# Attention scores over all 128 rows, another start order and other buffers for the conv weights

## The chip, the cores and the metric

The kernel runs on one core of a Trainium2 chip. The metric is the device time of one execution in microseconds (us), the median of three runs. The engines are called PE (TensorE, matrix products), DVE (VectorE), ACT (ScalarE), POOL (GpSimd) and SP (SyncE, which issues most loads). PEld is PE's loading of stationary weights.

## The reference, cut to what matters

One decoder block over 1024 tokens of width 1024: a combined projection, a gated short convolution and a sliding-window attention side by side, their gated sum, and a gated MLP with a convolution.

```python
u  = RMSNorm(x)
cb, cc, cx, q, k, v, g_conv, g_attn = split(u @ W_in + b_in)
y_conv = (cb * causal_dwconv3(cc * cx)) @ W_conv_out
y_attn = attention(rope(q), rope(k), v, sinks) @ W_attn_out + b
x = x + (sigmoid(g_conv) * y_conv + sigmoid(g_attn) * y_attn) @ W_mix_out
u  = RMSNorm(x)
up, gate = split(u @ W_up)
x = x + (silu(causal_dwconv3(up) + b) * gate) @ W_down
return RMSNorm(x)

# attention: 8 query heads, 2 key heads of 64; blocks of 128 queries;
# each block sees its own and the previous block of keys, band of 128
kk = concat([prev_block(k), k])            # block 0: the previous block is padding
scores = qb @ kk.T * 64 ** -0.5            # -inf outside the band and on the padding
m = max(max(scores), sink)
p = exp(scores - m); out = p / (sum(p) + exp(sink - m)) @ vv
```

## The kernel before

All arithmetic is float32. For PE each operand is split into a high part (an ACT cast) and a low part (a DVE subtraction), by `split`, and a product is three PE products, high by high, high by low and low by high (`mm3`, lines 144 to 146). So a weight tile of 128x1024 costs a load by SP into a buffer of the pool `rawp` (two buffers), a cast and a subtraction. Activation tiles of 128x1024 come from a pool of 16 buffers (`act`). Work runs in this order.

**The start** is written out by hand for all engines. For each of 8 blocks of 128 tokens, `rows_of(t)` makes the norm's statistics and the scaled rows y_a (five small DVE operations and one of 128x1024), and `cols_of(t)` turns them on PE (tp_a, line 182, 8 transposes) and splits the result into u. `part(name, qt)` (line 288) multiplies a weight tile (k, q0, q1) with 256 columns of u, 24 products; it needs two blocks of u. `turn_on(n)` lets the generator of the rotary angles go on by n operations, DVE ones first (lines 209 to 217), then 25 on POOL (lines 220 to 224), then DVE ones again. `keep_warm` runs products of zeros. In PSUM the accumulators of k, q0 and q1 (ps_k, ps_q) leave one place for tp_a.

**Attention** has 16 steps (8 query blocks by 2 key heads), `Step`, written out by hand for PE, ACT and DVE. Per step: a set of scores, four heads with two products each (lines 444 and 445); maxima with mask on DVE (451), exponentials on ACT, sums and normalised p on DVE (467); eight transposes of p (`turn`, 473); a split of these; four products with the values (483); then the head's output is summed and split into qs (`rest`, `total`, `store`). The first product of a score has the stationary qs[g], where the high and low part of one head's queries stand above each other in 64 rows each, and as moving side the high keys in both halves. The second has 64 rows, high queries by the low keys kl. Between a step's turn and its values PE runs half of a fill tile: 24 products with u (ps_fill), which make the attention gates and two tiles of the conv's input; DVE splits a fill weight in every second step.

**The attention output** (ya) multiplies W_ao with the attention's result, in the same tiles qs. After it comes the conv's in-projection with fewer products by a sum-and-difference scheme (zin, xin, yin), whose result z is stored to DRAM by column tiles.

**The conv output** (yc, line 144 ff. with co and z as operands) multiplies eight weight tiles co0 to co7 with z parts reloaded from DRAM (zr, halves of 512 tokens: z00 to z07, z10 to z17); the results are gated and merged (gm, line 917), split (m) and multiplied with eight mix weight tiles (mx). Here a scheduler sets the order, by when operands come and by the order of the code. Every weight tile and z part goes through the two buffers of `rawp`. Then come the MLP's up and down projections.

Of the kernel before, what the change touches and what calls it, by code (L numbers as in the profile page):

```python
# [72 lines left out]
def hybrid_kernel(ctx, tc, x, pos, cst, pcol, norms, w_in, w_ao, w_co, w_mix, w_up, w_down, out):  # L73
# [36 lines left out]
    def pc(i):  # L110
        return pcol_sb[:, i:i + 1]
# [129 lines left out]
    def turn_on(n=99):  # L241
        for _ in zip(range(n), angles):
            pass
# [32 lines left out]

    def cols_of(t, step=None):
        norm_cols(ys[t], u, t, f"a{t}", step)
# [12 lines left out]
    with tc.manual_schedule(engines={mybir.EngineType.PE, mybir.EngineType.Activation, mybir.EngineType.DVE, mybir.EngineType.SP, mybir.EngineType.Pool}):  # L291
        nc.vector.memset(eps, EPS)
        nc.scalar.activation(warm, eps, AF.Sqrt)
        nc.gpsimd.memset(zero, 0.0)
        keep_warm(N_WARM[0])
        load_x(0)
        nc.scalar.dma_start(posi, pos)
        nc.scalar.dma_start(cst_sb[:, CST_FREQ:CST_MASK], cst[:, CST_FREQ:CST_MASK])
        wb = act("nw0")
        nc.sync.dma_start(wb, norms[0:1, :].broadcast_to([P, D]))  # L300
        load_x(1)
        nc.sync.dma_start(cst_sb[:, :CST_FREQ], cst[:, :CST_FREQ])
# [21 lines left out]
        nc.sync.dma_start(cst_sb[:, CST_MASK:], cst[:, CST_MASK:])  # L324
        rows_of(2)
        turn_on(20)
        early["q0"] = split_unit(raw_q0, "q0")
        rows_of(3)
        part("k", 0)
        cols_of(2)  # L330
        early["q1"] = split_unit(raw_q1, "q1")
        rows_of(4)
        part("q0", 0)
        cols_of(3)
        rows_of(5)
        part("q1", 0)
        part("k", 1)
        cols_of(4)
        rows_of(6)
        part("q0", 1)  # L340
        cols_of(5)
        rows_of(7)
        turn_on(4)
        part("q1", 1)
        part("k", 2)
        cols_of(6)
        turn_on(7)
        part("q0", 2)
        cols_of(7)
        turn_on()  # L350
        part("q1", 2)
# [25 lines left out]

    own = [slice(0, HD), slice(HD, P)]
    other = [own[1], own[0]]
    qs = [mid(f"qs{g}", F32R) for g in range(2)]  # L380
    ks = [act(f"ks{g}", F32R) for g in range(2)]
    kl = act("kl", F32R)

    def rope_keys(part):
        k = rope(part)
        for g in range(2):
            split(k[own[g]], ks[g][own[g]], kl[own[g]])
        for g in range(2):
            nc.vector.tensor_copy(ks[g][other[g]], ks[g][own[g]].bitcast(F32))

    def rope_queries(part, c):
        q = rope(part)
        for g in range(2):
            split(q[own[g]], qs[g][own[g], c], qs[g][other[g], c])

    turn = {"k": rope_load(ps_early["k"], COL_BIN + U_K, "k")}
    for i in range(2):
# [24 lines left out]
    def fill_part(f, h, kcs):  # L422
        if h == 0 and kcs[0] == 0:
            ps_fill[f] = ps(f"ps_fill{f}")
        gemm_part(ps_fill[f], w_fill[f], u, halves[h], kcs)

    def fill_evict(f):
        col, alloc = fillers[f]
        filled[f] = alloc(f"fill{f}")
        return nc.scalar.activation(filled[f], ps_fill[f], AF.Identity, bias=pc(COL_BIN + col))  # L430

    class Step:
        def __init__(self, i):
            self.n, self.g = steps[i]
            self.name = f"{self.n}{self.g}"
            self.queries = slice(self.n * P, (self.n + 1) * P)

        def scores(self):
            rows, g = own[self.g], self.g
# [28 lines left out]

        def turn(self):
            self.pt = pt = ps(f"pt{self.name}", (P, 2, 4, P))  # L470
            for k2 in range(2):
                for c in range(4):
                    nc.tensor.transpose(pt[:, k2, c], self.p[:, c, k2 * P:(k2 + 1) * P], ident)

        def split(self):
            self.hl = [act(f"p{x}{self.name}", F32R, (P, 2, 4, P)) for x in "hl"]
            split(self.pt, *self.hl)
# [16 lines left out]

        def store(self):
            r = own[self.g]
            return split(self.os[r], qs[0][r, :, self.queries], qs[1][r, :, self.queries])

    for f in range(2):
        fill_split(f, load_unit(w_in[U_GA + f], f"fill{f}"))
# [11 lines left out]
    with tc.manual_schedule(engines={mybir.EngineType.PE, mybir.EngineType.Activation, mybir.EngineType.DVE}):  # L514
# [9 lines left out]
        for i, step in enumerate(st):  # L524
# [30 lines left out]
            if i == len(st) - 1:  # L555
                wa = [split_unit(raw_ao[0], "ao0")]
            step.values()
        st[-1].rest()
# [157 lines left out]
    v.scalar_tensor_tensor(c_0, ps_fill[9], pc(COL_BIN + U_X), c_0, op0=ALU.add, op1=ALU.mult)  # L716
    conv_taps(0, c_0)


    units_in = [(U_GC, U_B)]  # L720
# [55 lines left out]
    for q in range(4):  # L776
        if q > 1:
            wa.append(unit(w_ao[q], f"ao{q}"))
        if q > 1:
            next(gen_in)  # L780
            next(gen_in)
        if q == 3:
            pin.load(0)
            pin.prep(0, 3)
            pin.prep(0, 2)
        for jj in range(2):
            j = 2 * q + jj
            with tc.issue_after(after_attention):
                nc.scalar.activation(gas[j], gas[j], AF.Sigmoid)
            ya = ps(f"ya{j}")  # L790
            for cols in halves:
                for c in range(4):
                    f = slice((jj * 4 + c) * P, (jj * 4 + c + 1) * P)
                    mm3(ya[:, cols], wa[q][0][:, f], wa[q][1][:, f], qs[0][:, c, cols], qs[1][:, c, cols], c == 0, c == 3)
            v.scalar_tensor_tensor(ms[j], ya, pc(COL_BAO + j), gas[j], op0=ALU.add, op1=ALU.mult)
            nc.gpsimd.dma_start(msp[j], ms[j])
    wp.release()
    midp.release()
# [52 lines left out]
                3: [(2, lambda p: gate(p, bank("z"), pin.uv[p][:, 0]))]}.get(q, [])  # L851


    wco, zparts = {}, {}
# [12 lines left out]

    def tail_in(m):
        for f in {0: [lambda: load_co(0)], 1: [lambda: load_z(0, 0)], 2: [lambda: load_z(0, 1)], 3: [lambda: load_co(1)],
                  5: [lambda: load_co(2)], 6: [lambda: load_z(0, 2), lambda: load_z(0, 3)], 7: [lambda: load_co(3)]}.get(m, ()):  # L870
            f()

    pin.load(1)
# [446 lines left out]
```

## Time and profile before

| | |
|---|---|
| median of 3 runs | 1441.95 us (1440.77 to 1442.16) |
| profiled execution | 1441.58 us, span 1439.8 us |
| PE busy | 1418.2 us, 98% of the span |
| DVE busy | 1003.6 us, 70% |
| ACT busy | 562.5 us, 39% |
| POOL busy | 85.7 us, 6% |
| start, to the first 512-column product | 59.74 us |
| attention, first to last score | 109.6 to 255.6 us |
| conv and mix output | 601.7 to 710.9 us for the first 453 products |

The profile is of one execution; times in it count from the start of the span. [...] The granted clock is the share of full speed that PE was given.

### The profile page before, as it was taken

To read this page: it belongs to the slowest core of one execution; us is meant where nothing else is said; L and a number is where in the kernel's file an instruction comes from. 1 tells how busy PE (TensorE), PEld (TensorE's weight loads), DVE (VectorE), ACT (ScalarE), POOL (GpSimd) and SP (SyncE) were. 2 spreads that over 40 slices of the span, in tenths; PEclk is the share of its full clock that TensorE was granted. 3 is DMA by queue.
4 is the path that set the end of the run, shared out by engine and by line. 5 is a ranking of instruction groups with operands and counts; after the bars stand their busy time and mean duration, and the time that the engine had idled before them with its cause. 6 is when DMAs were issued, how large, how long until landed. Compare 5 with 4: busy or idle time off the path is not lost.

```text
span 1439.8 us, 17099 instructions
## 1 busy us (share of the span) xinstructions
PE 1418.2 (98%) x6447; PEld 1164.9 (81%) x6447; DVE 1003.6 (70%) x1511; ACT 562.5 (39%) x897; POOL 85.7 (6%) x144
## 2 busy tenths in 40 slices
PE   8999999999999999999999999999999999999997
PEld 6987777788888888877888878888888888888886
DVE  7575676856788787545644697787777777655567
ACT  5545555623333333232323543333333334444343
POOL 5210000000000000000000000000000000000000
PEclk9999999999999999999999999999999999999999
DMA  5320000242455554255552222222232225797603
GB/s 217 89 59 30 30 16 30 88 161 74 161 205 205 191 185 178 76 177 196 184 174 103 74 98 107 101 105 95 88 110 93 99 94 197 275 377 256 195 31 146
DMA packets 68450, 193.18 MB, mean 134 GB/s; under 512 B 8144, under 2 KB 8400, under 8 KB 68368
## 3 DMA queue, kind: packets, MB, share of 16 engines
q1 hardware_dynamic: 53280, 139.64, 28.8%
q0 software_dynamic: 14368, 51.13, 9.2%
q10 hardware_dynamic: 720, 1.33, 0.3%
q8 instruction: 50, 0.82, 0.2%
q14 instruction: 32, 0.26, 0.1%
HBM read 136.75 MB, written 52.69 MB: 132 GB/s over the span
## 4 chain that ended last, share of the span: by engine, by line
PE 86%; DVE 6%; DMA 5%; ACT 2%; issue 1%; SPq 0%; DVEq 0%; ACTq 0%
PE xup L649 8%; PE zup L649 8%; PE yup L649 8%; PE dna L1151 8%; PE dnb L1151 6%; PE yin L649 5%; PE xin L649 5%; PE zin L649 5%; PE wup L649 4%; PE win L649 3%; PE ps_fill L144 3%; PE ps_fill L146 3%; PE ps_fill L145 3%; PE mx L145 2%; PE mx L146 2%; PE mx L144 2%
## 5 line engine op out<-in xcount | busy, mean ns | idle before, releaser
L1138 DVE TENSOR_TENSOR pd<-rd,pd 128x1024 fp32r<-128x1024 f32 x77 | 93.7, 1222 | 54.1 <-ACT pd L1141 50.3
L627 ACT CAST pup<-sup 128x512 fp32r<-128x512 f32 x80 | 47.8, 620 | 203.2 <-DVE sup L613 203.2
L1141 ACT CAST pd<-rd 128x1024 fp32r<-128x1024 f32 x77 | 80.6, 1053 | 104.1 <-PE dnb L1151 37.1
L1151 PE MATMUL dna<-pd 128*128 128x512 f32 x528 | 120.3, 389 | 0.0
L1151 PEld LDWEIGHTS dna<-pd 128*128 128x128 f32 x528 | 99.1, 188 | 20.5
L1151 PE MATMUL dnb<-pd 128*128 128x512 f32 x396 | 90.2, 389 | 0.0
L1151 PEld LDWEIGHTS dnb<-pd 128*128 128x128 f32 x396 | 74.3, 188 | 15.4
L649 PE MATMUL zin<-u,pin 128*128 128x512 f32 x360 | 86.1, 389 | 0.0
L627 ACT CAST pin<-sin 128x512 fp32r<-128x512 f32 x52 | 31.1, 620 | 135.3 <-DVE sin L613 126.4
L649 PEld LDWEIGHTS zin<-u,pin 128*128 128x128 f32 x360 | 67.6, 188 | 14.0
L630 DVE TENSOR_TENSOR pup<-sup,pup 128x512 fp32r<-128x512 f32 x80 | 53.6, 689 | 18.5 <-ACT pup L627 15.0
L144 PE MATMUL ps_fill<-u,w_fill 128*128 128x512 f32 x160 | 64.0, 400 | 0.0
L146 PE MATMUL ps_fill<-u,w_fill 128*128 128x512 f32 x160 | 62.5, 391 | 0.0
L145 PE MATMUL ps_fill<-u,w_fill 128*128 128x512 f32 x160 | 62.3, 389 | 0.0
L649 PE MATMUL yup<-b22h,pup 128*128 128x512 f32 x176 | 57.9, 390 | 0.9 <-DVE aup L665 0.9
L649 PE MATMUL zup<-b11h,pup 128*128 128x512 f32 x176 | 57.8, 390 | 0.0
L649 PE MATMUL zup<-b21h,pup 128*128 128x512 f32 x176 | 57.7, 389 | 0.0
L451 DVE CUSTOM_DVE_ANT_0 p<-s,cst_sb,pcol_sb 128x256 f32<-128x256 f32 x64 | 27.2, 480 | 37.2 <-PE s L445 34.6
L649 PE MATMUL yup<-bt1h,pup 128*128 128x512 f32 x160 | 52.5, 389 | 0.0
L649 PE MATMUL wup<-bt2h,pup 128*128 128x512 f32 x160 | 52.5, 389 | 0.0
L649 PE MATMUL xup<-bt3h,pup 128*128 128x512 f32 x160 | 52.5, 389 | 0.0
L649 PE MATMUL xup<-bt4h,pup 128*128 128x512 f32 x160 | 52.5, 389 | 0.0
(361 smaller groups left out, 3470.4 us busy)
## 6 DMA issues: line engine op xcount, KB each, us to landing
rup<-in_w_up SPq DMA_DIRECT2D x44, 512.0 KB, 3.5
rin<-in_w_in SPq DMA_DIRECT2D x30, 512.0 KB, 6.7
td<-in_w_down SPq DMA_DIRECT2D x22, 512.0 KB, 5.3
tsp<-td POOLq DMA_DIRECT2D x22, 512.0 KB, 3.7
rd<-tsp SPq DMA_DIRECT2D x44, 256.0 KB, 5.3
rd<-in_w_down SPq DMA_DIRECT2D x33, 256.0 KB, 5.3
rd<-hs SPq DMA_DIRECT2D x33, 256.0 KB, 3.7
x<-in_x SPq DMA_DIRECT2D x16, 512.0 KB, 3.7
```

Of the source, the lines that this page charges most:

```text
L144: nc.tensor.matmul(dst, ah, bh, start=first, stop=False)
L145: nc.tensor.matmul(dst, ah, bl, start=False, stop=False)
L146: nc.tensor.matmul(dst, al, bh, start=False, stop=last)
L451: nc.vector.tensor_tensor_reduce(out=self.p[:, c], in0=self.s[:, c], in1=masks[0 if self.n == 0 else 1], scale=SCALE, scalar=pc(COL_SINK + ...
L627: nc.scalar.copy(self.parts[p, q][:, 0], src())
L630: v.tensor_sub(t[:, 1], src(), t[:, 0].bitcast(F32))
L649: nc.tensor.matmul(dst, a, b[:, kc], start=first and i == 0, stop=last and i == 2, skip_group_check=p >= PLAIN and more)
L1138: v.tensor_sub(t[:, 2:], raws_d[n - 1], t[:, :2].bitcast(F32))
L1141: nc.scalar.copy(parts_d[n][:, :2], raws_d[n])
L1151: nc.tensor.matmul(sets[side, i], t[:, s, tok], t[:, b], start=g == 0 and k == 0 and not more, stop=g == NG - 1 and k == 2, skip_group_che ...
```

## The change

1. **Scores.** The low keys become two tiles kl0 and kl1, one for each key head, of 128 rows; the other head's 64 rows are zeros, written once by POOL (two memsets of 64x1024). The second product of a score then runs over all 128 rows of qs[g], of which the zero rows add nothing.
2. **Queries by halves.** qs is laid out as halves of 512 tokens, then head, then token. W_ao's first group of products runs the first half for two output tiles and then the second half.
3. **First key block.** For query block 0 the two steps turn, split and multiply with the values only one key block (4 transposes and 2 value products a step instead of 8 and 4).
4. **First gate.** Fill 0 is stored to DRAM after its bias and reloaded later (ga0), which frees an activation buffer in between; the product that makes the conv's first input stands in the hand-written order, ahead of the last head's sum, and some work of the next stage is only issued after attention.
5. **Start.** x_1 is loaded ahead of the norm gains, q0's weights ahead of x_2. The first two blocks' norms come ahead of the angle operations; the first split of u comes behind eight of these; q0's weights are split ahead of block 2; the PE parts stand in another order.
6. **Conv weights.** co1 to co3 and z parts z00 to z03 are loaded into activation buffers and not through the two buffers of `rawp`.

```diff
+        load_x(1)
...
-        load_x(1)
         raw_k = load_unit(w_in[U_K], "k")
+        raw_q0 = load_unit(w_in[U_Q], "q0")
         load_x(2)
         load_x(3)
-        raw_q0 = load_unit(w_in[U_Q], "q0")
         load_x(4)
-        turn_on(2)
         rows_of(0)
-        turn_on(1)
         rows_of(1)
+        turn_on(8)
         cols_of(0, False)
         keep_warm(N_WARM[1])
+        early["k"] = split_unit(raw_k, "k", eng=nc.gpsimd)
         cols_of(0, True)
-        early["k"] = split_unit(raw_k, "k", eng=nc.gpsimd)
-        turn_on(5)
         cols_of(1)
+        turn_on(20)
...
-    qs = [mid(f"qs{g}", F32R) for g in range(2)]
+    qs = [mid(f"qs{g}", F32R, (P, 2, 4, 512)) for g in range(2)]
-    kl = act("kl", F32R)
+    kl = [act(f"kl{g}", F32R) for g in range(2)]
+    for g in range(2):
+        nc.gpsimd.memset(kl[g][other[g]].bitcast(F32), 0.0)
...
-                nc.tensor.matmul(self.s[:, c], qs[g][:, c, self.queries], ks[g][:, kc], start=True, stop=False)
-                nc.tensor.matmul(self.s[:, c], qs[g][rows, c, self.queries], kl[rows, kc], start=False, stop=True)
+                nc.tensor.matmul(self.s[:, c], qs[g][:, self.h, c, self.queries], ks[g][:, kc], start=True, stop=False)
+                nc.tensor.matmul(self.s[:, c], qs[g][:, self.h, c, self.queries], kl[g][:, kc], start=False, stop=True)
...
+            self.blocks = 2 if self.n else 1
-            for k2 in range(2):
+            for k2 in range(self.blocks):
                 for c in range(4):
                     nc.tensor.transpose(pt[:, k2, c], self.p[:, c, k2 * P:(k2 + 1) * P], ident)
...
-            for i in range(4):
-                nc.tensor.matmul(self.o, vs[self.g][:, n0 + i // 2], self.hl[i % 2][:, i // 2], start=i == 0, stop=i == 3)
+            n = 2 * self.blocks
+            for i in range(n):
+                nc.tensor.matmul(self.o, vs[self.g][:, n0 + i // 2], self.hl[i % 2][:, i // 2], start=i == 0, stop=i == n - 1)
...
+        if f == 0:
+            nc.gpsimd.dma_start(gsp0, filled[f])
...
+    gas[0] = act("ga0")
+    nc.sync.dma_start(gas[0], gsp0)
...
-        raw = load_unit(w_co[gr, hc], f"co{n}")
+        raw = raws_co.pop(n) if n in raws_co else load_unit(w_co[gr, hc], f"co{n}")
...
+    def fetch_co(n):
+        raws_co[n] = act(f"raw_co{n}")
+        nc.sync.dma_start(raws_co[n], w_co[n // 2, n % 2])
...
-        raw = rawp.tile([P, 512], F32, name=f"zr{th}{k}", tag="raw")
+        raw = rawp.tile([P, 512], F32, name=f"zr{th}{k}", tag="raw") if th or k > 3 else act(f"zr{th}{k}", F32, (P, 512))
```

The order of PE's work at the start, first before and then after. tp_a are the eight transposes of a token block (the order of the rows is that of blocks 2 to 6), ps_k, ps_q0 and ps_q1 the parts of 24 products; the first line is k's first part.

```order
L288 MATMUL ps_k_257<-u1_94,w_k_177 128x256 x24
L182 MATMUL tp_a2_282<-cst_sb_88,y_a2_212 128x128 x8
L288 MATMUL ps_q0_307<-u1_94,w_q0_243 128x256 x24
L182 MATMUL tp_a3_332<-cst_sb_88,y_a3_246 128x128 x8
L288 MATMUL ps_q1_354<-u1_94,w_q1_293 128x256 x24
L288 MATMUL ps_k_257<-u1_94,w_k_177 128x256 x24
L182 MATMUL tp_a4_403<-cst_sb_88,y_a4_296 128x128 x8
L288 MATMUL ps_q0_307<-u1_94,w_q0_243 128x256 x24
```

And after:

```order
L288 MATMUL ps_k_246<-u1_94,w_k_180 128x256 x24
L288 MATMUL ps_q0_282<-u1_94,w_q0_232 128x256 x24
L182 MATMUL tp_a2_307<-cst_sb_88,y_a2_235 128x128 x8
L182 MATMUL tp_a3_332<-cst_sb_88,y_a3_271 128x128 x8
L288 MATMUL ps_q1_343<-u1_94,w_q1_318 128x256 x24
L182 MATMUL tp_a4_379<-cst_sb_88,y_a4_321 128x128 x8
L288 MATMUL ps_k_246<-u1_94,w_k_180 128x256 x24
L182 MATMUL tp_a5_425<-cst_sb_88,y_a5_368 128x128 x8
L288 MATMUL ps_q0_282<-u1_94,w_q0_232 128x256 x24
```

q0's first part moved ahead of the turn of block 2, and k's second part behind the turn of block 4, so that the turns of blocks 2 and 3 follow each other and that of block 4 has one part ahead of it since block 3, not two.

The loads on SP at the entry of the conv output, first before and then after. raw_co are conv weight tiles, zr parts of z, gm gates for the merge.

```order
L121 DMA raw_co0_4601<-in_w_co 128x1024
L915 DMA gm00_4883<-gsp_2301 128x512
L916 DMA gm00_4883<-msp_2300 128x512
L864 DMA zr00_4624<-zsp_2302 128x512
L864 DMA zr01_4643<-zsp_2302 128x512
L121 DMA raw_co1_4661<-in_w_co 128x1024
L121 DMA raw_co2_4691<-in_w_co 128x1024
L864 DMA zr02_4699<-zsp_2302 128x512
L864 DMA zr03_4704<-zsp_2302 128x512
L121 DMA raw_co3_4712<-in_w_co 128x1024
L864 DMA zr04_4778<-zsp_2302 128x512
```

And after:

```order
L121 DMA raw_co0_4596<-in_w_co 128x1024
L880 DMA zr00_4619<-zsp_2298 128x512
L932 DMA gm00_4878<-gsp_2297 128x512
L933 DMA gm00_4878<-msp_2296 128x512
L876 DMA raw_co1_4624<-in_w_co 128x1024
L880 DMA zr01_4640<-zsp_2298 128x512
L876 DMA raw_co2_4645<-in_w_co 128x1024
L876 DMA raw_co3_4675<-in_w_co 128x1024
L880 DMA zr02_4693<-zsp_2298 128x512
L880 DMA zr04_4773<-zsp_2298 128x512
L880 DMA zr03_4701<-zsp_2298 128x512
L880 DMA zr05_4778<-zsp_2298 128x512
```

co1 to co3 (line 876 is the load into an activation buffer) moved up among the first z parts, and of the rows shown only co0, zr04 and zr05 still use the two buffers of `rawp`.

## Rows read from the trace of the kernel before

**Rows 1.** First part of the page: busy us (share) xinstructions, each engine.

```profile
PE 1418.2 (98%) x6447; PEld 1164.9 (81%) x6447; DVE 1003.6 (70%) x1511; ACT 562.5 (39%) x897; POOL 85.7 (6%) x144
```

**Rows 2.** Waits of PE: what waited for what, us in total, times, longest.

```profile
PE tp_a L182 <- DVE y_a L172: 3.6, 4, 1.6
PE yc L144 <- ACT co L138: 1.9, 1, 1.9
PE ps_k L288 <- DVE st_a L156: 1.5, 1, 1.5
...
PE yc L144 <- DVE gm L917: 1.1, 1, 1.1
PE ya L144 <- ACT qs L138: 1.0, 1, 1.0
```

**Rows 3.** Timeline of PE, one score set: start us, duration us, engine, line, operation.

```profile
117.60 0.28 PE L444 MATMUL s<-ks,qs 128*128 128x256 f32 x1
117.81 0.38 PE L445 MATMUL s<-kl,qs 64*128 64x256 f32 x1
118.12 0.39 PE L444 MATMUL s<-ks,qs 128*128 128x256 f32 x1
...
120.00 1.09 PE L473 MATMUL pt<-cst_sb,p 128*128 128x128 f32 x8
120.85 0.47 PE L144 MATMUL ps_fill<-u,w_fill 128*128 128x512 f32 x1
```

**Rows 4.** Chain that ended last, 35 to 45 us: start, us on it, what.

```profile
39.17 2.88 PE ps_k L288 x24
```

**Rows 5.** PEld, lines 445 and 288: duration ns minimum/median/maximum, first and last start.

```profile
L445 PEld LDWEIGHTS s<-kl,qs x64: 182/183/183, 109.8 to 255.6; 64*128 64x128 f32 x64
...
L288 PEld LDWEIGHTS ps_k<-u,w_k x96: 186/192/193, 13.8 to 52.0; 128*128 128x128 f32 x96
```

**Rows 6.** Timeline of PE, value products and the turn behind them, late in attention.

```profile
262.36 0.39 PE L483 MATMUL o<-ph,vs 128*128 128x512 f32 x1
...
263.27 1.03 PE L473 MATMUL pt<-cst_sb,p 128*128 128x128 f32 x8
264.06 0.48 PE L144 MATMUL ps_fill<-u,w_fill 128*128 128x512 f32 x1
```

**Rows 7.** Timeline of DVE over two attention steps; [ ] idle before and releaser.

```profile
178.37 0.48 DVE L451 CUSTOM_DVE_ANT_0 p<-s,cst_sb,pcol_sb 128x256 f32<-128x256 f32 x1 [1.50 <-PE s L445]
...
184.27 1.22 DVE L467 TENSOR_TENSOR p<-p,sm 128x1024 f32<-128x1024 f32 x1
188.08 0.48 DVE L451 CUSTOM_DVE_ANT_0 p<-s,cst_sb,pcol_sb 128x256 f32<-128x256 f32 x1 [2.58 <-PE s L445]
...
195.01 1.22 DVE L139 TENSOR_TENSOR w_fill<-raw_fill,w_fill 128x1024 fp32r<-128x1024 f32 x1
```

**Rows 8.** Windows: us, busy us (x) PE, PEld, DVE, ACT, POOL, clock, DMA.

```profile
10.00:25.00 15.00, 11.43 (x83) 9.33 (x81) 14.55 (x24) 9.90 (x15) 10.20 (x9) 1.00 0.79 296
150.00:200.00 50.00, 50.00 (x230) 38.62 (x228) 35.50 (x92) 28.46 (x68) 0.00 (x0) 1.00 0.11 32
601.70:710.90 109.20, 105.65 (x453) 85.10 (x451) 55.78 (x73) 34.30 (x46) 1.06 (x2) 0.98 0.56 183
630.00:640.00 10.00, 8.61 (x31) 6.96 (x32) 3.83 (x4) 3.33 (x4) 0.00 (x0) 0.83 0.50 157
```

**Rows 9.** Timeline of PE in the conv output, behind its longest wait.

```profile
631.39 0.55 PE L144 MATMUL yc<-z,co 128*128 128x512 f32 x1 [1.92 <-ACT co L138]
631.74 0.63 PE L145 MATMUL yc<-z,co 128*128 128x512 f32 x1
...
634.72 0.58 PE L146 MATMUL yc<-z,co 128*128 128x512 f32 x1
```

**Rows 10.** Timeline of DVE at the start, from one block's statistics to the next's.

```profile
26.22 0.14 DVE L156 TENSOR_SCALAR st_a<-ss_a 128x1 f32<-128x1 f32 x1
...
30.33 0.14 DVE L156 TENSOR_SCALAR st_a<-ss_a 128x1 f32<-128x1 f32 x1
```

More of the change, by code (lines that the diff above doesn't have):

```diff
@@ L324, in hybrid_kernel @@
         nc.sync.dma_start(cst_sb[:, CST_MASK:], cst[:, CST_MASK:])
+        early["q0"] = split_unit(raw_q0, "q0")
         rows_of(2)
-        turn_on(20)
-        early["q0"] = split_unit(raw_q0, "q0")
+        part("k", 0)
         rows_of(3)
-        part("k", 0)
+        part("q0", 0)
         cols_of(2)
@@ L332, in hybrid_kernel @@
         rows_of(4)
-        part("q0", 0)
         cols_of(3)
+        part("q1", 0)
         rows_of(5)
-        part("q1", 0)
+        cols_of(4)
         part("k", 1)
-        cols_of(4)
         rows_of(6)
+        cols_of(5)
         part("q0", 1)
-        cols_of(5)
         rows_of(7)
-        turn_on(4)
+        cols_of(6)
         part("q1", 1)
[L345 to L348, printed above, removed]
         cols_of(7)
         turn_on()
+        part("k", 2)
+        part("q0", 2)
         part("q1", 2)
@@ L386, in rope_keys @@
         for g in range(2):
-            split(k[own[g]], ks[g][own[g]], kl[own[g]])
+            split(k[own[g]], ks[g][own[g]], kl[g][own[g]])
         for g in range(2):
@@ L393, in rope_queries @@
         for g in range(2):
-            split(q[own[g]], qs[g][own[g], c], qs[g][other[g], c])
+            split(q[own[g]].rearrange("p (h t) -> p h t", h=2), qs[g][own[g], :, c], qs[g][other[g], :, c])
     turn = {"k": rope_load(ps_early["k"], COL_BIN + U_K, "k")}
@@ L425, in fill_part @@
         gemm_part(ps_fill[f], w_fill[f], u, halves[h], kcs)
+    gsp0 = dram.tile([P, T], F32, name="gsp0")
     def fill_evict(f):
@@ L429, in fill_evict @@
         filled[f] = alloc(f"fill{f}")
-        return nc.scalar.activation(filled[f], ps_fill[f], AF.Identity, bias=pc(COL_BIN + col))
+        nc.scalar.activation(filled[f], ps_fill[f], AF.Identity, bias=pc(COL_BIN + col))
+        if f == 0:
+            nc.gpsimd.dma_start(gsp0, filled[f])
     class Step:
@@ L435, in __init__ @@
             self.name = f"{self.n}{self.g}"
-            self.queries = slice(self.n * P, (self.n + 1) * P)
+            self.h, self.queries = self.n // 4, slice(self.n % 4 * P, (self.n % 4 + 1) * P)
+            self.blocks = 2 if self.n else 1
         def scores(self):
-            rows, g = own[self.g], self.g
+            g = self.g
             w0 = max(0, self.n - 1) * P
@@ L476, in split @@
             self.hl = [act(f"p{x}{self.name}", F32R, (P, 2, 4, P)) for x in "hl"]
-            split(self.pt, *self.hl)
+            split(self.pt[:, :self.blocks], *[x[:, :self.blocks] for x in self.hl])
         def values(self):
@@ L498, in store @@
             r = own[self.g]
-            return split(self.os[r], qs[0][r, :, self.queries], qs[1][r, :, self.queries])
+            return split(self.os[r], qs[0][r, self.h, :, self.queries], qs[1][r, self.h, :, self.queries])
     for f in range(2):
@@ L715, in hybrid_kernel @@
     c_0 = filled[8]
-    v.scalar_tensor_tensor(c_0, ps_fill[9], pc(COL_BIN + U_X), c_0, op0=ALU.add, op1=ALU.mult)
-    conv_taps(0, c_0)
+    with tc.issue_after(after_attention):
+        conv_taps(0, c_0)
     units_in = [(U_GC, U_B)]
@@ L779, in hybrid_kernel @@
         if q > 1:
-            next(gen_in)
-            next(gen_in)
+            with tc.issue_after(after_attention):
+                next(gen_in)
+                next(gen_in)
         if q == 3:
-            pin.load(0)
-            pin.prep(0, 3)
-            pin.prep(0, 2)
+            with tc.issue_after(after_attention):
+                pin.load(0)
+                pin.prep(0, 3)
+                pin.prep(0, 2)
+        yas = [ps(f"ya{2 * q + jj}") for jj in range(2)]
+        for jj, h in [(jj, h) for h in range(2) for jj in range(2)] if q == 0 else [(jj, h) for jj in range(2) for h in range(2)]:
+            for c in range(4):
+                f = slice((jj * 4 + c) * P, (jj * 4 + c + 1) * P)
+                mm3(yas[jj][:, halves[h]], wa[q][0][:, f], wa[q][1][:, f], qs[0][:, h, c], qs[1][:, h, c], c == 0, c == 3)
         for jj in range(2):
@@ L789, in hybrid_kernel @@
                 nc.scalar.activation(gas[j], gas[j], AF.Sigmoid)
[L790 to L795, printed above, removed]
+            v.scalar_tensor_tensor(ms[j], yas[jj], pc(COL_BAO + j), gas[j], op0=ALU.add, op1=ALU.mult)
             nc.gpsimd.dma_start(msp[j], ms[j])
@@ L868, in tail_in @@
     def tail_in(m):
-        for f in {0: [lambda: load_co(0)], 1: [lambda: load_z(0, 0)], 2: [lambda: load_z(0, 1)], 3: [lambda: load_co(1)],
-                  5: [lambda: load_co(2)], 6: [lambda: load_z(0, 2), lambda: load_z(0, 3)], 7: [lambda: load_co(3)]}.get(m, ()):
+        for f in {0: [lambda: load_co(0)], 1: [lambda: load_z(0, 0), lambda: fetch_co(1)], 2: [lambda: load_z(0, 1), lambda: fetch_co(2)],
+                  3: [lambda: load_co(1)], 4: [lambda: fetch_co(3)],
+                  5: [lambda: load_co(2), lambda: load_z(0, 2)], 6: [lambda: load_z(0, 3)], 7: [lambda: load_co(3)]}.get(m, ()):
             f()
```

3 lines of the change are left out of this document (2 added, 1 removed).

## The prediction

> **What bounds the kernel now.** I read the busy line first: TensorE (PE) is busy 98% of the span, VectorE (DVE) 70%, GpSimd (POOL) 6% [rows 1]. So the time is PE's instruction stream plus its few waits, and an edit counts only if it shortens that stream, removes a wait of PE or makes one. The list of PE's waits comes next [rows 2]. Its longest lie in stages that the change touches: the start (tp_a 3.6, ps_k 1.5), the attention output (ya 1.0), the conv output (yc 1.9 and 1.1). Attention itself has no wait there, so in it I look for slow PE instructions. A timeline of one score set shows them [rows 3]: eight products of 256 columns take 120.00 − 117.60 = 2.40 us, 0.31 from one to the next. Elsewhere products with as many columns, all over 128 rows, stream 24 in 2.88 us, 0.12 each [rows 4].
>
> **Scores over 128 rows.** In each set a 128-row and a 64-row product alternate [rows 3]; the change makes all eight 128-row. Nothing of the trace but the switch of rows tells the two kinds of stream apart: both load new weights for each product, 183 or 192 ns a load [rows 5], yet only the alternating one pays more than the columns need. I take the pitch of the full-row stream: 8 × 0.12 = 0.96 us a set, and 16 sets × (2.40 − 0.96) = **−23.0 us**. The bounds: nothing gained (pitch 0.31), and −23.0; a pitch equal to the load, 0.19, would give 16 × (2.40 − 1.52) = −14. The row nearest in kind is [rows 4], hence the end. The eight transposes behind a set take 0.85 [rows 3], those behind full-row values 0.79 [rows 6]: 15 × 0.06 = **−0.9**.
>
> [...]
>
> The padding is two memsets of 64x1024 on POOL, which is 6% busy, well ahead of the first score; if they slowed DVE beside them, nothing in PE's dense stretch hangs on it. Nothing is added on PE: the instructions keep their number.
>
> **What a shorter attention step asks of DVE.** A step on PE now is 24 fill products, four value products, a score set and a turn: 5.5 + 0.91 [rows 6] + 2.40 + 0.85, about 9.7; after it 5.5 + 0.91 + 0.96 + 0.79 = 8.2. From the end of the scores to the normalised p DVE and ScalarE (ACT) need 178.37 → 185.49 = 7.1 us, and p is turned behind the next score set, 8.2 later: 1.1 to spare. In every second step DVE also splits fill weights, to 196.23, 8.15 after that step's maxima began at 188.08 [rows 7]; the next maxima are due at 8.2. A slip there is small and the lighter step takes it up. DVE's load, 35.5 of 50 us [rows 8], becomes 35.5 × 9.7/8.2 = 42 of 50. So the gain stays on PE. Not hidden: 0; bound 0 to +8 (half a microsecond a step, the second rival).
>
> **First key block left out.** In two steps four transposes (0.79/8 = 0.10 each) and two of four value products (0.23 each) go: 2 × (0.40 + 0.46) = **−1.7**. The two split operations get shorter on engines that wait anyway.
>
> **Attention output.** W_ao's queries by halves let 24 products run before block 7's queries are needed; PE already does as many before its wait of 1.0 at the same point, since the scheduler interleaved the halves. The wait ends with DVE's last sum, which stands behind the same five long operations after as before. **0**, bounds −1.0, the whole wait, to +0.5. The first gate's store to DRAM and reload use POOL's and SP's queues over 200 us before its sigmoid: 0.
>
> **Conv output.** The window 601.7 to 710.9 holds 453 products [rows 8]; at the value products' 0.2275 [rows 6] they need 103.1 of 109.2 us, so 6.1 are lost: waits of 1.9 and 1.1 [rows 2], some smaller ones, and, behind the 1.9, a stretch where the granted clock is 0.83 on average [rows 8] and eight products stand 0.43 apart [rows 9], the lower of the two levels, 1.5 lost. The 1.9 is the fifth weight tile's: its load had to wait for one of two raw buffers, each held by load, cast and subtraction of the tile before. After, tiles 1 to 3 and z parts 0 to 3 use free activation buffers, so the chain through the two raw buffers is four tiles and four z parts shorter. Adding loads and splits by their times in this trace, the tightest is tile 6, whose raw buffer waits for z part 6: it comes about 2 us before its use. The 1.1 (gm) is a PSUM bank not yet evicted; the first bank now finishes 12 products apart from the next instead of all bunched, so it goes. What is late next is mix weight 7, whose split now stands behind one more merge on DVE: I leave 0.3 of wait. **−5.8**, bounds −6.1 and 0.
>
> **Start.** Here the change costs. DVE is busy 14.55 of the 15 us from 10 to 25 [rows 8]; a row block costs it 26.22 → 30.33 = 4.1 us beside POOL (statistics, scaling, the u subtraction) [rows 10], against 2.88 + 0.85 on PE [rows 3, 4]. The two first blocks' norms now go ahead of the angles, but the first u subtraction moves behind eight angle operations, q0's split ahead of block 2. By these durations k's last third starts at 16.5 (before 17.7), q0's first part ends at 20.8, tp_a 3 waits to 23.2, and tp_a 4, which needs the one free PSUM pair and so the u subtraction of block 3, waits from 27.6 to 29.8. Before, PE had q1 and k's second part to do there. Queued behind it is all of PE. At the end of q1's second part and tp_a 7 I get 42.7 against 40.9 for the same work before: **+1.8**. If the waits inside hide as well as now, −1; if each of tp_a 3 to 7 waits as long as the longest of the kind now, 1.6 [rows 2], about +4.5.
>
> **Sum.** −23.0 − 0.9 − 1.7 − 5.8 + 1.8 = −29.6. The profiled execution had 1441.58 with a span of 1439.8, so 1412.0 with a span of 1410.2; it lies 0.4 under the median, and the median goes to **1412.3 us**.
>
> **Rivals.**
> 1. *Full-row pairs do not stream:* the pitch stays 0.31. For it: the first product of a set, which follows full rows, stands 0.21 before the next, not 0.12 [rows 3]. Against it: [rows 4]. What is left is −1.7 − 5.8 + 1.8 = −5.7: 1436. Chance 0.05.
> 2. *DVE and ACT become attention's bound*, about 8.7 a step: one more wait of DVE for ACT in each chain. For it: slack of only 0.05 in the heavy steps [rows 7]. Against: 1.1 in the others. 16 × 0.5 = +8: 1420. Chance 0.13.
> 3. *The conv loads are late all the same*, or mix weight 7 is, with the lower clock behind it: none of the 5.8 is won: 1418. Chance 0.13.
> 4. *The start loses 4.5 or gains 1*: 1409 to 1415, in the forecast's range.
> 5. *Slower than before:* in attention PE waits in each step and the clock falls to the lower level behind each wait, as behind the 1.9 in [rows 9], 1.5 each time. It decides from 29.6/16 = 1.85 a step, a wait of 0.35 with the fall; with a wait of 1.0, 16 × 2.5 = 40: 1452. Against it: the waits of 1.5 at the start and 1.1 at gm [rows 2] have no such stretch behind them. Chance 0.02.
>
> **How the numbers follow.** Forecast with its own spread (start, conv remainder, turn) 1407 to 1416: chance 0.67. Rivals 2 and 3 lie at 1418 and 1420, and can meet in part. The range that leaves out about 2 in 10 (rival 1, rival 5, the two together, a conv or start better than every bound) is 1405.5 to 1421. About 0.2%, 2.9 us, is what a measurement of this kernel can tell from no change: faster 0.96 (forecast, rivals 1 to 4), same 0.02 (rival 1 with a bad start), slower 0.02 (rival 5).
>
> **What the changed profile would show.** Score sets: eight products in about 1.0 us, second products 128-row. Steps: 8.2 from value products to value products, no PE wait on p, pl or fill weights; a wait there is rival 2. Start: PE waits of 1.5 and 2.2 at tp_a 3 and 4, the first 512-column q2 product near 61.5, not 59.7. Conv: no wait for co, 453 products in 103.5 us and a granted clock of 1.00 throughout. I am wrong if the score pitch is over 0.15, or if attention's step is over 8.5.

## The result and the profile after

The changed kernel took 1417.2 us in the median of four executions (1415.16 to 1418.96), the kernel before on the same chip 1441.75 us (1440.77 to 1442.16). The ratio is 0.983, with an interval from 0.9813 to 0.9847. The forecast was 1412.3 us with a range from 1405.5 to 1421: of the 29.6 us that it took off, 24.6 came.

The profiled execution of after had 1418.96 us, a span of 1417.2: it is the slowest of the four. The same kernel was profiled once more (the last experiment), and that execution had 1413.86 us, a span of 1412.1. Both are in the table, since they differ in two places only, and those two are what the forecast missed. Stages run from the first product of one kind to the first of the next: start (to the first 512-column q2 product), the rest of the queries (to the first score), attention (to the first product of the attention output, ya), ya and in-projection (to the first of yc), yc (to the first of mx), mx (to the first of the up projection), the rest.

| stage | before | forecast | after, profiled | after, second profile |
|---|---|---|---|---|
| start | 59.74 | +1.8 | 66.21 (+6.47) | 62.41 (+2.67) |
| rest of the queries | 49.88 | 0 | 49.91 (0) | 49.91 (0) |
| attention | 160.88 | −25.6 | 135.09 (−25.79) | 135.11 (−25.77) |
| ya and in-projection | 331.06 | 0 | 330.62 (−0.44) | 330.63 (−0.43) |
| yc | 98.97 | −6.1 | 92.48 (−6.49) | 92.48 (−6.49) |
| mx | 93.05 | +0.3 | 96.71 (+3.66) | 95.32 (+2.27) |
| rest | 646.22 | 0 | 646.18 (0) | 646.24 (0) |
| span | 1439.8 | 1410.2 | 1417.2 (−22.6) | 1412.1 (−27.7) |

(The forecast's −5.8 for the conv output was −6.1 of waits and lower clock gone and 0.3 of new wait for mix weight 7; the 0.3 falls into the stage mx.)

The busy line of after answers to [rows 1]: PE has 12 instructions less (the first key block) and 24 us less, its share is unchanged.

```profile
PE 1394.5 (98%) x6435; PEld 1161.0 (82%) x6435; DVE 1002.1 (71%) x1511; ACT 561.9 (40%) x897; POOL 86.2 (6%) x147
```

The waits of PE in after answer to [rows 2].

```profile
PE tp_a L182 <- DVE st_a L156: 3.1, 2, 1.9
PE ps_k L288 <- DVE u L139: 2.7, 1, 2.7
PE mx L144 <- ACT mx L138: 1.7, 1, 1.7
PE ps_q L288 <- DVE u L139: 1.6, 1, 1.6
...
PE ya L144 <- ACT qs L138: 0.9, 1, 0.9
PE mx L145 <- DVE mx L139: 0.8, 1, 0.8
```

The two yc waits of [rows 2], 1.9 and 1.1, are gone, and nothing of attention is in the list. New are a wait of 2.7 at the start and one of 1.7 for the last mix weight; another for that weight is now 0.8, where before had 0.2. A score set in the timeline of PE answers to [rows 3]; its last row is the first of the eight transposes behind the set.

```profile
178.28 0.28 PE L450 MATMUL s<-ks,qs 128*128 128x256 f32 x1
178.39 0.28 PE L451 MATMUL s<-kl,qs 128*128 128x256 f32 x1
...
179.11 0.28 PE L451 MATMUL s<-kl,qs 128*128 128x256 f32 x1
179.23 0.27 PE L479 MATMUL pt<-cst_sb,p 128*128 128x128 f32 x1
```

Eight products take 179.23 − 178.28 = 0.95 us, 0.12 each, where they took 2.40. The duration in a row, 0.28, is longer than that: the rows overlap, so what a product costs is read here from one start to the next. The next set begins 8.22 later. The windows of after (us, busy us and instructions of PE, PEld, DVE, ACT, POOL, granted clock, DMA) answer to [rows 8]: the first is attention's, the others are the start, the entry of mx and the yc stage.

```profile
150.00:200.00 50.00, 50.00 (x269) 43.10 (x268) 41.02 (x100) 32.72 (x84) 0.00 (x0) 1.00 0.11 32
18.00:26.00 8.00, 7.84 (x44) 7.84 (x45) 6.25 (x14) 0.16 (x1) 7.37 (x8) 0.61 0.54 208
...
680.00:700.00 20.00, 17.58 (x71) 13.87 (x70) 10.23 (x19) 4.86 (x8) 0.53 (x1) 0.91 0.44 151
...
581.83:674.31 92.48, 92.48 (x409) 76.58 (x408) 48.03 (x62) 29.12 (x40) 1.05 (x2) 1.00 0.53 174
```

PE is busy in all 50 us of attention with DVE at 41.0, and through the whole yc stage at full clock, where [rows 8] had a stretch of 10 us with 8.61 busy and a clock of 0.83. At the start and at mx the granted clock is a mean over stretches of two levels: shorter windows of after show 0.50 from 18 to 24 and from 687 to 689.5, 1.00 from 25 to 30 and from 690 to 700 (in before, behind the wait of 1.92 in [rows 9], 0.50 from 632 to 635). The second profile of the same kernel shows 1.00 in the windows of the start and of mx:

```profile
18.00:26.00 8.00, 6.39 (x49) 5.75 (x50) 7.72 (x16) 2.53 (x3) 7.38 (x8) 1.00 0.55 214
...
680.00:700.00 20.00, 17.77 (x77) 14.28 (x77) 11.87 (x25) 5.68 (x10) 1.06 (x2) 1.00 0.47 168
```

PE is busier in the first profile (7.84 against 6.39 of 8 us) and yet does fewer instructions (44 against 49): a lower clock looks like a busy engine, and only the count beside it shows the difference.

### The profile page after: what moved, and what is told of

Read it like the earlier page. It is cut to its first block, busy times and chain, and to the rows that moved or that the text cites. A ratio compares the mean times of both kernels' runs of the same rounds, so it can differ in the third digit from the quotient of the medians.

```text
span 1417.2 us, 17090 instructions
## 1 busy us (share of the span) xinstructions
PE 1394.5 (98%) x6435; PEld 1161.0 (82%) x6435; DVE 1002.1 (71%) x1511; ACT 561.9 (40%) x897; POOL 86.2 (6%) x147
## 4 chain that ended last, share of the span: by engine, by line
PE 87%; DVE 5%; DMA 4%; ACT 2%; issue 1%; SPq 0%; DVEq 0%; ACTq 0%
PE xup L659 8%; PE zup L659 8%; PE yup L659 8%; PE dna L1168 8%; PE dnb L1168 6%; PE yin L659 6%; PE xin L659 6%; PE zin L659 6%; PE wup L659 4%; PE win L659 3%; PE ps_fill L146 3%; PE ps_fill L144 3%; PE ps_fill L145 3%; PE mx L145 2%; PE mx L146 2%; PE mx L144 2%
## 5 line engine op out<-in xcount | busy, mean ns | idle before, releaser
L144 PE MATMUL mx<-mx,m 128*128 128x512 f32 x128 | 50.8, 397 | 1.7 <-ACT mx L138 1.7
```

The costliest lines, as they stand in the source:

```text
L144: nc.tensor.matmul(dst, ah, bh, start=first, stop=False)
```

## The experiments

**One part at a time.** The first three kernels ask which part of the change moved which stage. In the first, the start alone is put back as it was:

```diff
-        turn_on(8)
+        turn_on(2)
         rows_of(0)
+        turn_on(1)
         rows_of(1)
...
-        part("q0", 0)
         cols_of(2)
+        part("q0", 0)
```

> The changed kernel with the start of the kernel before. If the start alone is what fell short of the forecast, the first q2 product is back from 66.2 to about 59.7 us and the time goes from 1417.2 to about 1410.7 (the forecast without its start term: 1410.5). If instead the two first stages share the loss (the attention work only moved it), the time stays above 1414.

It took 1414.36 us (1412.3 to 1414.68), ratio 0.9803 (0.9788 to 0.9817). Its start is 59.70 against 59.74 before, its span 1410.5, and all other stages are those of after to 0.15 us. So the changed start is a loss by itself. Without its +1.8 the forecast's sum is −31.4 and its span 1408.4; of the 2.1 above that, mx makes 3.2 (+3.54 for 0.3), and the other stages won 1.1 more than forecast.

In the second the conv loads are put back as well, so that attention's edits stand alone (here and in the next, one of the lines put back; the others are in the diff of the change):

```diff
-        raw = raws_co.pop(n) if n in raws_co else load_unit(w_co[gr, hc], f"co{n}")
+        raw = load_unit(w_co[gr, hc], f"co{n}")
```

> The start and the conv loads of the kernel before, the rest of the change kept (scores over 128 rows, queries by halves, first key block, first gate by way of DRAM). If the attention edits are worth what the two traces show between the first q2 product and the first conv product (-25.8 and -0.6), 1415.4. If part of it was bought by the other edits (buffers, order), more than 1419. The conv waits of 1.9 and 1.1 with the lower clock behind should be back.

It took 1415.2 us (1414.4 to 1415.86), ratio 0.9811 (0.9795 to 0.9828). Attention is 135.08, the yc stage 99.20, and the waits of PE for co and gm are back:

```profile
PE yc L144 <- ACT co L138: 2.4, 1, 2.4
PE yc L144 <- DVE gm L933: 1.3, 2, 1.1
```

There is no wait for mix weights here, and mx takes 92.34. So both the gain in yc and the loss in mx belong to the conv loads. The third has the conv loads alone, on the kernel before:

```diff
+        raw = raws_co.pop(n) if n in raws_co else load_unit(w_co[gr, hc], f"co{n}")
-        raw = load_unit(w_co[gr, hc], f"co{n}")
```

> The kernel before with the conv weights and z parts by activation buffers, nothing else. Theory: the conv part itself brings its 5.8, and takes back 3 at the mix weights (mix weight 7 split behind the late merges, waits of 1.7 and 0.8 and the lower clock): 1441.8 - 2.7 = 1439. Rival: the wait at mix weight 7 comes from the other edits, and the conv part alone brings 5.8: 1436.

It took 1437.92 us (1436.24 to 1440.66), ratio 0.997 (0.996 to 0.9981). The yc stage is 92.48, −6.49 as in after, and mx 94.86, +1.81, with the new waits:

```profile
PE mx L144 <- ACT mx L138: 1.1, 1, 1.1
...
PE mx L145 <- DVE mx L139: 0.8, 1, 0.8
```

The edit wins 6.5 us and gives back 1.8 in the next stage, with no attention edit in the kernel. (Its span is 3.6 shorter, not 4.7, since its start, which no edit touched, took 60.47, 0.7 more than before, and ya and in-projection 0.3 more.)

**Why the scores were slow.** The forecast named the switch between 128 and 64 rows; by its first rival, products of 128 rows behind each other would keep the pitch of 0.31. On the kernel before, the order of the products is changed to two of 128 rows, two of 64, and so on; rows, loads and columns stay:

```diff
-            for c in range(4):
-                ...(ks...) ; ...(kl...)
+            for cs in ((0, 2), (1, 3)):
+                for c in cs: ...(ks...)
+                for c in cs: ...(kl...)
```

> The kernel before, each set of scores in the order two 128-row, two 64-row, two 128-row, two 64-row products: four switches of rows a set and not eight. If the switch is what costs (0.31 at a switch, 0.12 without), a set takes 4 x 0.12 + 4 x 0.31 = 1.72 us and not 2.40, 16 sets gain 10.9: 1431. If every 64-row product has its load in series whatever stands before it, a set takes 2 x 0.12 + 6 x 0.31 = 2.10: 1437. [...]

A single execution took 1428.69 us against 1441.78 for the median of before; what follows is read from its stages. A score set of it in the timeline of PE:

```profile
170.24 0.40 PE L445 MATMUL s<-ks,qs 128*128 128x256 f32 x2
170.57 0.50 PE L447 MATMUL s<-kl,qs 64*128 64x256 f32 x2
171.00 0.50 PE L445 MATMUL s<-ks,qs 128*128 128x256 f32 x2
171.43 0.50 PE L447 MATMUL s<-kl,qs 64*128 64x256 f32 x2
171.86 0.87 PE L475 MATMUL pt<-cst_sb,p 128*128 128x128 f32 x6
```

The set takes 171.86 − 170.24 = 1.62, not 2.40. Each later pair takes 0.43, which is what one product behind its like at 0.12 and one switch at 0.31, the pitch of [rows 3], add up to; the first pair, 0.33, is 0.12 and the 0.21 at the head of [rows 3]. Sixteen sets give 16 × 0.78 = 12.5 us, and attention is 148.31 long, −12.57. The same eight weight loads are in it, so the loss went with the number of switches and not with that of loads. What a switch adds, 0.31 − 0.12 = 0.19, is as long as one load (0.18 to 0.19 in [rows 5]); what happens at a switch no run shows.

**What holds the start.** In the timeline of PE, the start of after (answering to [rows 4] and to the forecast's steps) is:

```profile
18.16 2.08 PE L288 MATMUL ps_k<-u,w_k 128*128 128x256 f32 x8 [2.72 <-DVE u L139]
20.04 4.89 PE L288 MATMUL ps_q<-u,w_q 128*128 128x256 f32 x24
24.77 1.91 PE L182 MATMUL tp_a<-cst_sb,y_a 128*128 128x128 f32 x16
```

k's last third begins at 18.16, not at 16.5, behind a wait of 2.72 for u; then 24 products take 24.77 − 20.04 = 4.73 us, where [rows 4] has 2.88. The wait has its cause on DVE; the timeline of POOL (first row) and of DVE ahead of it:

```profile
10.45 2.79 POOL L139 TENSOR_TENSOR w_k<-raw_k,w_k 128x1024 fp32r<-128x1024 f32 x1 [9.20 <-ACT w_k L138]
...
10.94 2.33 DVE L209 CAST posf<-posi 128x8 f32<-128x8 int32 x1
13.31 0.42 DVE L210 TENSOR_TENSOR rt<-posf,cst_sb 128x256 f32<-128x256 f32 x1
```

A cast of eight elements a partition takes 2.33 us and ends at 13.27, with POOL's subtraction of k's low part (10.45 + 2.79 = 13.24); the whole chain of angle operations and with it u stands behind it. One kernel puts another operation in that place:

```diff
+        turn_on(1)
         rows_of(0)
         rows_of(1)
-        turn_on(8)
+        turn_on(7)
```

> The changed kernel with one DVE operation moved: the cast of the positions (line 209, 128x8), which took 2.33 us beside POOL's subtraction for w_k, goes ahead of the first block's statistics. Theory (the cast itself was slow, or slow at that place only): all DVE work behind it is 2.3 earlier, k's last third starts at about 15.9 and not 18.2, and the start is 2.3 to 4 shorter (the lower clock behind that wait goes too): first q2 product at 62 to 64. Rival (whichever DVE operation of that kind follows waits until POOL's subtraction ends at 13.2): line 210 or 213 takes the 2.3 us instead, the u subtractions end at the same 18.1, and the first q2 product stays at 66.

It took 1416.83 us (1416.73 to 1418.25), ratio 0.9832 (0.9816 to 0.9848): nothing won. Its start is 62.25 with a clock of 1.00, k's last third at 17.97; but mx takes 98.59, with a clock of 0.83 from 680 to 700. In the timeline of DVE the next operation is held in the cast's place, to 13.54, with POOL's subtraction ending at 13.25:

```profile
10.96 2.58 DVE L210 TENSOR_TENSOR rt<-posf,cst_sb 128x256 f32<-128x256 f32 x1
```

So it is not the cast that is slow. Not every DVE operation is held beside POOL, though. Later in the start of after, beside another two-input operation of POOL (first row), a one-input operation of 128x1 takes its usual 0.15, and a two-input one 0.43 where it takes 0.22 alone, ending with POOL's at 19.90:

```profile
18.77 1.13 POOL L223 TENSOR_TENSOR rt<-rt 128x256 f32<-128x256 f32 x1
...
19.29 0.15 DVE L157 RECIPROCAL st_a<-st_a 128x1 f32<-128x1 f32 x1
19.47 0.43 DVE L159 SCALAR_TENSOR_TENSOR st_a<-st_a 128x1 f32<-128x1 f32 x1
```

The next kernel takes POOL's subtraction away instead, and has DVE make it:

```diff
-        early["k"] = split_unit(raw_k, "k", eng=nc.gpsimd)
+        early["k"] = split_unit(raw_k, "k")
```

> The changed kernel with w_k's low part subtracted by DVE, behind the eight angle operations, and not by POOL. POOL is then idle until 15 us. If POOL's subtraction is what held up the DVE operation beside it (2.33 us at line 209 in the changed kernel, 2.50 at line 213 in the kernel before), no DVE operation between 10 and 14 us takes over 0.5 us; DVE gains 2.2 and pays 1.2, k's last third starts near 17 and the start is about 1 to 3 shorter. If the slow operation is the cast itself, it stays at 2.3 and the start gets longer by 1.2.

It took 1412.46 us (1412.32 to 1413.72), ratio 0.9801 (0.9786 to 0.9815). In the timeline of DVE the cast now takes 0.17, and the subtraction costs 1.22:

```profile
10.91 0.17 DVE L209 CAST posf<-posi 128x8 f32<-128x8 int32 x1
...
13.56 1.22 DVE L139 TENSOR_TENSOR w_k<-raw_k,w_k 128x1024 fp32r<-128x1024 f32 x1
```

The start is 60.68, with k's last third at 17.11. With POOL idle the hold is gone, and with it 1.7 to 1.8 of the start's loss of 2.7 (62.41 and 62.46 in the two kernels with the unchanged start and no fall of the clock).

**The clock behind the wait.** One theory was that the clock falls because PE waits 2.72 us idle. So twelve products of zeros were put into the wait:

```diff
+            if name == "k" and qt == 0 and (a, b) == (1, 0):
+                keep_warm(12)
```

> The changed kernel with 12 products of zeros (0.22 us each) in PE's 2.7 us wait ahead of k's last third; nothing else. If the lower clock from 18 to 26 us is brought on by that wait, the products there run at 0.12 and not 0.24 each, tp_a 2 comes 2.7 us earlier, and the first q2 product moves from 66.2 to 62 to 64, since DVE and ACT get block 2 earlier as well. If the start is set by DVE alone, the products wait for DVE again at tp_a 3 and 4 and the first q2 product stays within 1 us of 66.2.

It took 1413.38 us (1411.95 to 1416.35), ratio 0.9808 (0.9793 to 0.9822). The start is 61.84 with a clock of 1.00 throughout it, though k's last third begins at 18.17 as in after. (The profiled execution is the slowest of the four, 1416.35: its loss is at mx, 98.39, with a clock of 0.83 from 680 to 700.) No fall at the start fits the theory, but the early cast's kernel kept a wait of 2.50 and had no fall either (start 62.25). So the unchanged kernel was run again, with more executions:

> The changed kernel once more, unchanged. Theory: its stages are fixed but for the granted clock, which falls behind the waits at the start (3.8 us where it does) and at mx (up to 3) in some executions only: times from 1414 (no fall) to 1420 (both), median near 1417, the lower the mean clock the longer, and in the profile the conv stage is 92.5 and attention 135.1 again, while the start is either near 62.4 or near 66. Rival: the start of 66.2 is what this order always gives, and the run on mix weights 0 to 3 had another start for a reason of its own: then 66 again.

Five executions took 1413.19 to 1418.71 us, median 1414.85, ratio 0.9829 (0.9815 to 0.9843). The profiled one has the identical wait and no fall behind it:

```profile
18.17 1.21 PE L288 MATMUL ps_k<-u,w_k 128*128 128x256 f32 x8 [2.72 <-DVE u L139]
19.22 3.04 PE L288 MATMUL ps_q<-u,w_q 128*128 128x256 f32 x24
22.34 1.09 PE L182 MATMUL tp_a<-cst_sb,y_a 128*128 128x128 f32 x8
24.61 1.09 PE L182 MATMUL tp_a<-cst_sb,y_a 128*128 128x128 f32 x8 [1.18 <-DVE y_a L172]
...
30.50 1.09 PE L182 MATMUL tp_a<-cst_sb,y_a 128*128 128x128 f32 x8 [1.23 <-DVE st_a L156]
```

So the wait is not sufficient. Nor is one as long necessary: behind the shorter wait of 1.92 in before the clock was at 0.50 as well, and with before's start, whose waits are shorter (2.1 at most there), the kernel with attention's edits alone had a granted clock of 0.79 from 18 to 26 (start 59.96), and the one with the conv loads alone 0.84 from 10 to 18 (60.47), which cost 0.2 and 0.7 us. Over the nine executions the mean granted clock goes with the time: 0.998 and 0.997 for 1413.86 and 1413.19, 0.993 for 1418.71 and 1418.96. What decides in one execution that the clock falls behind such a wait isn't settled here.

**The last mix weight.** The timelines of after around the entry of mx, of SP's queue, DVE, ACT and PE:

```profile
647.21 20.55 SPq L121 DMA_DIRECT2D raw_mx<-in_w_mix  x8
...
679.84 0.32 SPq L932 DMA_DIRECT2D gm<-gsp  x1
...
682.52 0.69 DVE L934 TENSOR_TENSOR gm<-yc,gm 128x512 f32<-128x512 f32 x1 [2.11 <-DMA gm<-gsp]
...
684.05 0.62 ACT L138 CAST m<-gm 128x512 fp32r<-128x512 f32 x1 [2.91 <-DVE gm L935]
684.57 1.04 ACT L138 CAST mx<-raw_mx 128x1024 fp32r<-128x1024 f32 x1
...
685.66 0.51 PE L144 MATMUL mx<-mx,m 128*128 128x512 f32 x1 [1.67 <-ACT mx L138]
686.92 0.80 PE L145 MATMUL mx<-mx,m 128*128 128x512 f32 x1 [0.76 <-DVE mx L139]
687.52 0.63 PE L146 MATMUL mx<-mx,m 128*128 128x512 f32 x1
687.94 0.63 PE L144 MATMUL mx<-mx,m 128*128 128x512 f32 x1
```

SP issues all eight mix loads in a row, which takes 20.55 us because each waits for one of two raw buffers. The last is issued at 667.4 and lands at 671.1, yet ACT casts it only at 684.57: on ACT that cast stands behind the merges' casts (m). The last of these waits 2.91 for its merge, and the merge 2.11 on DVE for its gate, whose load SP issued at 679.84, 12 us after the last mix load, when the split of an earlier merge had freed its buffer. So the mix weight was there in time, and SP's row of loads was not what held that gate. In the kernel before, the same cast (first row) starts as its load lands, and 12 of the 16 merges' casts stand ahead of it, not 14:

```profile
705.53 1.05 ACT L138 CAST mx<-raw_mx 128x1024 fp32r<-128x1024 f32 x1 [1.40 <-DMA raw_mx<-in_w_mix]
708.41 0.62 ACT L138 CAST m<-gm 128x512 fp32r<-128x512 f32 x1 [1.83 <-DVE gm L918]
```

With attention's edits alone it is 12 too, with no wait; in every kernel with the conv loads and the mix loads as they were it is 14, with a wait of 1.1 to 2.0. PE loses 1.67 and 0.76 in after, and, in this execution, six products at 0.43 (687.52 on) instead of 0.23. How much a lower clock adds differs: over the seven profiles of such kernels mx is longer than before by 1.8, 2.3 and 2.6 where the clock stays at 1.00, and by 3.5, 3.7, 5.3 and 5.5 where it falls. In one kernel the first four mix weights are loaded into activation buffers:

```diff
-        raw = load_unit(w_mix[n // 2, n % 2], f"mx{n}")
+        if n < 4:
+            raw = act(f"raw_mx{n}")
+            nc.sync.dma_start(raw, w_mix[n // 2, n % 2])
+        else:
+            raw = load_unit(w_mix[n // 2, n % 2], f"mx{n}")
```

> The changed kernel with the raw tiles of mix weights 0 to 3 in activation buffers, so that the eight loads no longer stand one behind the other ahead of the gates (gm12 on) and mix weight 7's split comes ahead of merge 15's on DVE and ACT. If the waits of 1.7 and 0.8 at mx and the lower clock behind them are what the stage from the first mix product to the MLP lost, it goes from 96.7 back to 93.0 or less, and the conv stage ahead of it stays at 92.5: 1413.5. Rival: the merges themselves are late, because the conv stage is 6.5 shorter with the same loads; then the wait moves to m (merge 12 to 15) and the stage stays above 95: 1416.

It took 1411.89 us, all four executions between 1411.87 and 1411.92; ratio 0.9795 (0.9778 to 0.9811). Of the two waits one is left, and mx takes 93.43:

```profile
681.25 0.50 PE L145 MATMUL mx<-mx,m 128*128 128x512 f32 x1 [0.78 <-DVE mx L139]
```

The edit changes the order on ACT too: the casts of the last two mix weights, at 675.58 and 677.95, now stand ahead of the merges' casts at 681.83 and 683.16, with 13 merges' casts ahead of the last. That this order is what won fits the traces; no run changes the order alone.

**Better versions.** The kernel with before's start and the four mix loads joins the first and the last finding:

> The start of the kernel before and the mix weights as in the run on mix weights 0 to 3: the parts of the change that gain, without the two that lose. Sum of the stages: 59.7 + 49.9 + 135.1 + 330.6 + 92.5 + 93.0 + 646.2 = 1407.0 of span, 1408.8; if the mix weights bring nothing, 1412.4.

It took 1408.65 us (1408.21 to 1409.74), ratio 0.9773 (0.9759 to 0.9788), with a span of 1406.8. That beats both kernels, the one before by 33 us, and the changed one by 6 to 9 (its medians were taken on other chips). Its start is 59.71 and mx 92.87. The other way, keeping the changed start but with k's subtraction on DVE, five products of zeros in the wait and the four mix loads,

```diff
+                keep_warm(5)
...
-        early["k"] = split_unit(raw_k, "k", eng=nc.gpsimd)
+        early["k"] = split_unit(raw_k, "k")
...
+            raw = act(f"raw_mx{n}")
```

> The changed start with w_k's subtraction on DVE and 5 products of zeros in the wait ahead of k's last third, and mix weights 0 to 3 in activation buffers. First q2 product at 60.7 as without the zeros, if the clock stays up in every execution; span 1408.0, 1409.8. If the zeros only matter where the clock fell, the times of the runs lie within 1.5 of each other, against 3.8 for the changed kernel.

took 1411.31 us (1411.04 to 1412.31), ratio 0.9792 (0.9777 to 0.9807). The start is 61.22, and a wait of 1.4 for a fill on DVE, seen in no other kernel, makes the in-projection's stage 332.32. Expected were 60.7 and 1409.8: the changed start is not mended by this.

## Why the prediction was right, and where it was off

The median of 1417.2 lies above the forecast's own spread of 1407 to 1416. It lies in the range because that reached up to rivals 2 and 3, at 1420 and 1418, of which the one did not come and the other came in part; two mis-sized terms filled that room, which is luck. The second five executions, with 1414.85, lie in the spread.

- **Scores over 128 rows: right.** A set takes 0.95 where 0.96 was forecast, the step 8.22 (8.2). With the transposes and the first key block the stage came to −25.8 for −25.6. The scores make 16 × 1.45 = 23.2 of it and leave 2.6 for those two, as forecast; no run tests them apart. The rival in which full-row pairs don't stream is refuted twice: by these sets, and by the pairs on the kernel before, where four switches fewer in a set, with the same loads, won 0.78. Full-row products, each with its own load of 0.19 (190 and 191 ns on average for lines 450 and 451 of after), follow each other at 0.12.
- **DVE in attention: right, with little to spare.** The rival of 8.7 a step did not come: PE is busy for 50.00 of 50 us, with DVE at 41.0 (42 forecast). The chain from the first maximum to the normalised p is short enough and the slack in the heavy steps is 0.20 us, seen in these two rows of DVE in after, which answer to [rows 7]:

```profile
186.24 1.22 DVE L139 TENSOR_TENSOR w_fill<-raw_fill,w_fill 128x1024 fp32r<-128x1024 f32 x1
187.65 0.48 DVE L457 CUSTOM_DVE_ANT_0 p<-s,cst_sb,pcol_sb 128x256 f32<-128x256 f32 x1 [0.20 <-PE s L451]
```

- **Attention output: right**, a wait of 0.9 stayed where 1.0 was. The stage behind it won 0.44, which no term had; its cause was not looked for.
- **Conv output: right** in yc, −6.49 where 6.1 was the most that was thought to be lost there; no wait for co, a clock of 1.00. The stage is 92.48 in every kernel with these loads.
- **Mix weight 7: mis-sized.** The forecast left it 0.3, from one more merge on DVE ahead of its split. It measured +2.27 without and +3.66 with a lower clock behind it, +1.81 with the conv edit alone, and up to +5.5 in other kernels. The step that failed was to count only DVE, and no fall of the clock: on ACT the weight's cast came to stand behind two more merges, the last of them late, 13.5 us after its load had landed. The third rival named it and gave it the whole 5.8; where the clock fell longest, that was nearly so.
- **Start: mis-sized.** Forecast +1.8, with a bound of +4.5; measured +2.67 and, with the lower clock, +6.47, outside the bound. Two things were missing. The hold of a DVE operation by POOL's subtraction: k's last third began 1.7 later than worked out (18.17 for 16.5), q0 ended at 22.3 for 20.8, tp_a 3 came at 24.6 for 23.2, tp_a 4 at 30.5 for 29.8, so that 0.9 of it was left at the end. And a price for the clock: the forecast had one for the rival of attention, from [rows 9], but none for the start, because the wait of 1.5 there had no fall behind it in before. The hold stands in the trace of before, in rows that the prediction did not use: the same subtraction on POOL (first row) holds an angle operation there:

```profile
12.52 2.36 POOL L139 TENSOR_TENSOR w_k<-raw_k,w_k 128x1024 fp32r<-128x1024 f32 x1 [11.27 <-ACT w_k L138]
...
12.66 2.50 DVE L213 TENSOR_TENSOR rt<-rt 128x256 f32<-128x256 f32 x1
```

The sum of the profiled execution: forecast −29.6, measured −22.6. Of the 7.0 between them the start is 4.7 and mix weight 7 is 3.4; the other stages won 1.1 more than forecast. With the clock at its full level at both places (the second profile) it was −27.7, and with mix weight 7 mended, 1411.89 us, 0.4 from the forecast. There two errors cancel: the start lost 0.9 more than forecast, and attention, ya and yc together won 1.0 more.

## What to carry to other kernels

A stream of matrix products that alternates two row counts paid at each switch here: pad the smaller one with zeros, or at least bring like ones together; eight products went from 2.40 to 0.95 us by the one and to 1.62 by the other. When a load is moved to a free buffer, follow the order of work on every engine, to the next stage: with what was gained at one wait (6.5 us) came an order on ACT in which a cast that was ready stood behind others that were not (1.8 to 5.5 lost). And a moved step has to be looked at beside what the other engines do in its new place: here a cast that takes 0.17 us alone took 2.33 beside a subtraction of 2.79 on POOL.

## What the runs showed of the hardware

- **A switch between 128 and 64 rows** costs 0.31 us from product to product for 256 columns, against 0.12 between likes, and 0.21 at the first switch of a set.
- **Some DVE operations that started beside a two-input operation on POOL lasted until that ended, or up to 0.29 us longer**: 2.33 us for a cast of 128x8 that takes 0.17 with POOL idle, 2.58 for a two-input operation of 128x256 that takes 0.42, and 0.43 for one of 128x1 that takes 0.22. A one-input operation of 128x1 was not held (0.15). Beside a one-input operation of POOL (17.83 to 18.68 in after), a two-input DVE operation of 128x1024 that started at 18.02 took 1.28 us, against 1.22 in attention with POOL idle. What decides which operation is held no run shows.
- **The same wait of 2.72 us on PE** was followed by a granted clock of 0.61 in one execution and of 1.00 in another of the same kernel. Its nine executions spread from 1413.19 to 1418.96 us, while the four of the kernel with the smaller mx wait lay within 0.05 us, with the same wait at the start.
